# Two norms of an encoder trunk: buffers for the squares, held conditioning chunks, and a fused modulation on VectorE

## The chip, the core and the metric

One core of a Trainium2 chip runs the whole program. The metric is the device time of one execution in microseconds (us), lower is better. TensorE (PE in the profile, PEld where it loads weights) multiplies matrices, VectorE (DVE) and ScalarE (ACT) work on elements, SyncE (SP) issues the DMAs that bring the weights.

## What is computed

A trunk of two layers over 256 tokens of width 1024, all in float32. Each layer is a token mixer and then a feed-forward part, and ahead of each stands a norm whose scale and shift come from a conditioning vector `c`. Cut to what matters here:

```python
def adaln(x, g, shift, scale):
    return rmsnorm(x, g) * (1 + scale[:, None, :]) + shift[:, None, :]
...
    for l in range(DEPTH):
        mod = jax.nn.silu(c) @ ada_w[l] + ada_b[l]
        sh_m, sc_m, g_m, sh_f, sc_f, g_f = jnp.split(mod, 6, axis=-1)
        hn = adaln(x, mix_norm_g[l], sh_m, sc_m)
        ...                                   # four kinds of attention on hn @ w_in[l]
        x = x + g_m[:, None, :] * y
        hn = adaln(x, ffn_norm_g[l], sh_f, sc_f)
        if l % 2 == 0:
            f = swiglu(hn, ffn_w1[l // 2], ffn_w3[l // 2], ffn_w2[l // 2])
        else:
            f = moe_swiglu(...)               # router, 8 experts
        x = x + g_f[:, None, :] * f
    return rmsnorm(x, final_norm_g)
```

## The kernel before, in words

**Layout and precision.** The residual stream `xT` lies transposed in SBUF, eight pieces `xT[:, k]` of 128 channels by 256 tokens. Each float32 operand of a large product is split into a rounded part and the rest (`hi` and `lo` of weights, `hnh` and `hnl` of the normed stream), and `mm3` (matmuls on L102) makes three products of them: hi with hi, lo with hi, hi with lo. A weight comes in loads of 1 MB into a ring of six buffers `raw`; ACT rounds it (`CAST`, L76) and DVE takes the rest (L81), 1024 columns at a time, into four buffers.

**A norm edge.** Between a product and the next one that needs the normed stream stands this chain. DVE adds the gated product to `xT` (L735, eight steps). ACT squares each piece (`Stats.add`, L272); the squares go in pairs into two buffers `sq`, so the fifth square waits until the first pair has been summed. PE sums each square over the channels, two matmuls with one column `mean` per piece. A matmul here of float32 operands stands in the trace as two of half the work, so 16 sums are 32 rows there. From the sums `rsqrt` makes `rtok` (L255 to L259, two steps on ACT, three on DVE), and `Stats.rstd` (L288) spreads it over the partitions with PE, into PSUM. Then `scaled` (L294, DVE) multiplies `xT[:, k]` by it into `hn`, and `modulate` makes of each `hn` the rounded `hnh` (L315, ACT), the same unrounded (L316, ACT) and their difference `hnl` (L317, DVE), with scale `modA` (from `gain`, L303) and shift from `mods`.

There are three such edges and the MoE's own norm: edge 0 at the start, edge 1 between the first mixer and the dense feed-forward part, edge 2 between that and the second mixer.

**Conditioning chunks.** The product of `silu(c)` with `ada_w` is cut into chunks of 512 columns, spread over the program (`Beside.step`): two loads of 1 MB each, and either 32 small matmuls on PE (L215, `pj<-raw,cq`) or, `summed`, eight steps on DVE (L206 and seven of L208) and four matmuls. Each then takes a copy on ACT (L218), a transpose on PE (L219) and an addition on DVE (L221) into `mods`. At edge 1 `beside.upto(0, 10)` makes the chunk whose result `gain` needs; the first summed chunk of the dense part stands close behind it.

**Order.** Each engine runs its instructions in one fixed order. It is set ahead of time by a scheduler that takes instructions as their operands become ready in its own simulated time; `after(inst)` (L62) holds an instruction back behind another. So a local edit can move instructions elsewhere. The dense part is 11 steps of `hidden` (products with `w1` and `w3`) and `down` (with `w2`); the eight experts of the second layer follow much later (from 590 us).

Of the kernel before, what the change touches and what calls it, by code (L numbers as in the profile page):

```python
# [10 lines left out]
F32 = mybir.dt.float32  # L11
# [9 lines left out]
P = 128  # L21
# [18 lines left out]
def trunk(ctx, tc, I, out):  # L40
# [53 lines left out]
    class Acc:  # L94
# [4 lines left out]
            self.first = True  # L99

        def mm(self, o, lhsT, rhs, stop=False):
            pe.matmul(o, lhsT, rhs, start=self.first, stop=stop, skip_group_check=True)  # L102
            self.first = False

        def mm3(self, o, s, m, stop=False):
            self.mm(o, s[0], m[0])
# [44 lines left out]
    class Ada:  # L151
# [33 lines left out]
        def step(self):  # L185
            m, kh, w = self.load()
            for r in range(4):
                self.add(m, cz[:, kh * 4 + r], w[:, r], not self.todo and r == 3)
            if not self.todo:
                self.finish()  # L190

    class Beside:
# [3 lines left out]
            self.todo = list(chunks)  # L196
            self.tag = "pj"

        def step(self, summed=False):

            l, m = self.todo.pop(0)
            ws = [load(rows(I["ada_w"][l], kh * 512, 4, m * 512, m * 512 + 512), 4, 512) for kh in range(2)]
            w = [ws[k // 4][:, k % 4] for k in range(KC)]
            v = main.tile([P, 512], F32, name="ada", bufs=2)
            if summed:
                dve.tensor_scalar_mul(v, w[0], cs[:, 0:1])  # L206
                for k in range(1, KC):
                    dve.scalar_tensor_tensor(v, w[k], cs[:, k:k + 1], v, op0=ALU.mult, op1=ALU.add)  # L208
                terms = [(oz, v)]
            else:  # L210
                terms = [(cq[:, k], w[k]) for k in range(KC)]
            b = bank(self.tag)
            for i, (z, x) in enumerate(terms):
                for j in range(4):
                    pe.matmul(b[32 * j:32 * j + 32, :P], z, x[:, j * P:j * P + P], start=(i == 0),  # L215
                              stop=(i == len(terms) - 1), skip_group_check=True, tile_position=(0, 32 * j))
            v = v[:, :P]
            act.copy(v, b[:, :P])  # L218
            pe.transpose(b[:, P:2 * P], v, ident)  # L219
            a = S_AB + 48 * l + 4 * m  # L220
            dve.tensor_add(mods[l][:, m], b[:, P:2 * P:32], sm[:, a:a + 4])  # L221

        def upto(self, l, m):

            while self.todo and self.todo[0] < (l, m):
                self.step()

    beside = Beside([(0, m) for m in range(4, 12)] + [(1, m) for m in range(12)])
    owed = [0]

    def fill(n=1, summed=False):

        owed[0] += n
        while owed[0] >= 2:
            owed[0] -= 2
            if beside.todo:
                beside.step(summed)

    def mod(l, i):
        return mods[l].rearrange("p m j -> p (m j)")[:, 8 * i:8 * i + 8]  # L240
# [21 lines left out]
    class Stats:  # L262
# [3 lines left out]
            self.nk, self.n, self.tag, self.ms = nk, 0, tag, Acc(tag)  # L266

        def add(self, x):
            if self.n % 2 == 0:
                self.sq = main.tile([P, 2 * T], F32, name="sq", bufs=2)  # L270
            sq = self.sq[:, self.n % 2 * T:][:, :T]
            self.last = act.activation(sq, x, AF.Square)  # L272
            self.n += 1
            for t in range(2):
                self.ms.mm(self.ms.t[:, t:t + 1], sq[:, t * P:t * P + P], mean, self.n == self.nk)

        def tokens(self):

# [12 lines left out]
    def scaled(rstd, dst=None):  # L291
        for k in range(KC):
            t = main.tile([P, T], F32, name="hn", bufs=4) if dst is None else dst[:, k]
            dve.tensor_mul(t, xT[:, k], rstd)  # L294
            yield t
# [33 lines left out]
    def run(steps):  # L329
        for _ in steps:  # L330
            pass

    def ada(chunks):
        a = Ada(0, chunks, "sc")
        while a.todo:
            a.step()
# [19 lines left out]
    def mixer(l, wk, ts):  # L356
        w_in = I["w_in"][l]
        lam_init = 0.8 - 0.6 * math.exp(-0.3 * l)
        (hh, hl), edge = halves(), []
        adaln = modulate(l, S_MG + 8 * l, 0, 1, ts, hh, hl, edge, l == 0)  # L360
        if l == 0:
            ada(range(0, 4, 2))
            next(adaln)
        else:
            run(adaln)

        def hx(k, t0=0, t1=T):
            return hh[:, k, t0:t1], hl[:, k, t0:t1]
# [369 lines left out]
            yield st, k  # L738

    def normed(steps):  # L740
        for st, _ in steps:
            pass
        return scaled(st.rstd())

    def mix_out(l, oTh, oTl, tag=None):
        accs = [Acc("pj") for _ in range(4)]
# [9 lines left out]

    def dense(l, wk, ts):
        (hh, hl), edge = halves(), []
        run(modulate(l, S_FG + 8 * l, 3, 4, ts, hh, hl, edge))
        accs = [Acc(t) for t in ("sc", "sc", "tp", "tp")]  # L760
        ys = [accs[k // 2].t[:, (k % 2) * T:(k % 2) * T + T] for k in range(KC)]
        nst = D_FF // 256
# [31 lines left out]
        for s in range(nst):  # L794
            if s + 1 < nst:
                hidden(s + 1)
            down(s)
            fill(1 if s > 7 else 2, True)
        beside.upto(1, 4)
        return add_gated(ys, mod(l, 5), "pj")  # L800

    with tc.tile_pool(name="wk", bufs=1) as wk:
        mq = wk.tile([P, 8, T], F32, name="mq")
        dve.memset(mq, 0.0)
        o = mixer(0, wk, xn)
        beside.upto(0, 6)
        ts = normed(mix_out(0, *o, "tp"))
        beside.upto(0, 10)
        ts = normed(dense(0, wk, ts))
        o = mixer(1, wk, ts)  # L810
        beside.upto(1, 6)

# [461 lines left out]
```

## Time and profile before

| | |
|---|---|
| median of three executions | 1616.28 us (1615.56 to 1616.67) |
| the profiled execution | 1615.89 us, of which the span of the trace is 1614.1 |
| edge 0 | 0 to 30 us |
| first mixer | 30 to 181.5 us |
| edge 1 | 181.5 to 205 us |
| dense feed-forward part | 205 to 393.5 us |
| edge 2 | 393.5 to 407 us |
| experts | 590 to 1600 us |

The stages are read from the timeline by their lines. The profiled execution is 0.39 us below the median. Where PE is busy all through a stage, the stage ends when PE is done; where PE stands idle, another engine or a transfer sets the time.

### The profile page before, as it was taken

To read this page: it belongs to the slowest core of one execution; us is meant where nothing else is said; L and a number is where in the kernel's file an instruction comes from. 1 tells how busy PE (TensorE), PEld (TensorE's weight loads), DVE (VectorE), ACT (ScalarE), POOL (GpSimd) and SP (SyncE) were. 2 spreads that over 40 slices of the span, in tenths; PEclk is the share of its full clock that TensorE was granted. 3 is DMA by queue.
4 is the path that set the end of the run, shared out by engine and by line. 5 is a ranking of instruction groups with operands and counts; after the bars stand their busy time and mean duration, and the time that the engine had idled before them with its cause. 6 is when DMAs were issued, how large, how long until landed. Compare 5 with 4: busy or idle time off the path is not lost.

```text
span 1614.1 us, 24569 instructions
## 1 busy us (share of the span) xinstructions
PE 1550.2 (96%) x9449; PEld 1314.0 (81%) x9449; DVE 1301.3 (81%) x1840; ACT 1062.0 (66%) x1470; POOL 49.0 (3%) x48
## 2 busy tenths in 40 slices
PE   6999999999999969899999999999999999999997
PEld 5998899999998858787787888878887878788785
DVE  4786577776696489799889999888988888888887
ACT  3666454344766468677677777777777777676775
POOL 0000000000001010000000000000000001000000
PEclk8999899999999979999999999999999999999999
DMA  9874477886573549999989999989998989999992
GB/s 349 308 248 168 160 261 266 299 303 207 185 265 121 207 166 352 319 368 324 349 319 347 370 373 318 385 311 339 363 365 315 378 286 361 338 368 338 354 317 84
DMA packets 224396, 478.31 MB, mean 296 GB/s; under 512 B 11664, under 2 KB 39440, under 8 KB 224272
## 3 DMA queue, kind: packets, MB, share of 16 engines
q1 hardware_dynamic: 224272, 476.68, 82.7%
q8 instruction: 75, 1.23, 0.3%
q14 instruction: 49, 0.40, 0.1%
HBM read 475.60 MB, written 1.05 MB: 295 GB/s over the span
## 4 chain that ended last, share of the span: by engine, by line
PE 53%; DVE 4%; issue 1%; ACT 1%; POOL 0%; ACTq 0%; DVEq 0%
PE pj L102 33%; PE sc L102 17%; DVE mlo L81 2%; PE tp L1026 1%; DVE lo L81 1%; PE tp L102 1%; DVE acc L1072 1%; POOL ada L1063 0%; DVE rs L1059 0%; DVE ada L112 0%; ACT hi L76 0%; ACT mhi L76 0%; PE tp L998 0%; DVE sq L1020 0%; DVE raw L1185 0%
## 5 line engine op out<-in xcount | busy, mean ns | idle before, releaser
L81 DVE TENSOR_TENSOR lo<-raw,hi 128x1024 fp32r<-128x1024 f32 x352 | 423.4, 1223 | 69.1 <-ACT hi L76 63.9
L76 ACT CAST hi<-raw 128x1024 fp32r<-128x1024 f32 x354 | 364.9, 1048 | 102.8 <-PE pj L102 50.6
L81 DVE TENSOR_TENSOR mlo<-raw,mhi 128x1024 fp32r<-128x1024 f32 x224 | 268.4, 1229 | 17.7 <-ACT mhi L76 15.8
L76 ACT CAST mhi<-raw 128x1024 fp32r<-128x1024 f32 x224 | 229.2, 1050 | 39.4 <-PE pj L102 22.8
L102 PE MATMUL pj<-hnh,hi 128*128 128x256 f32 x640 | 182.9, 287 | 3.1 <-ACT hnh L315 2.2
L102 PE MATMUL pj<-hnl,hi 128*128 128x256 f32 x640 | 180.5, 283 | 1.0 <-DVE hnl L317 0.9
L102 PE MATMUL pj<-hnh,lo 128*128 128x256 f32 x640 | 179.2, 282 | 0.3 <-DVE lo L81 0.3
L102 PE MATMUL sc<-hi,ada 128*128 128x512 f32 x448 | 146.6, 398 | 1.6 <-DVE ada L112 1.3
L81 DVE TENSOR_TENSOR mlo<-more,mhi 128x1024 fp32r<-128x1024 f32 x112 | 135.7, 1238 | 14.7 <-ACT mhi L76 14.0
L81 DVE TENSOR_TENSOR lo<-more,hi 128x1024 fp32r<-128x1024 f32 x110 | 131.4, 1220 | 16.8 <-ACT hi L76 9.5
L102 PE MATMUL sc<-mhi,ada 128*128 128x512 f32 x432 | 139.6, 394 | 5.5 <-DVE ada L112 4.1
L76 ACT CAST mhi<-more 128x1024 fp32r<-128x1024 f32 x112 | 115.5, 1051 | 26.6 <-PE pj L102 17.8
L76 ACT CAST hi<-more 128x1024 fp32r<-128x1024 f32 x110 | 113.0, 1050 | 27.4 <-PE pj L102 9.9
L102 PEld LDWEIGHTS pj<-hnh,hi 128*128 128x128 f32 x640 | 121.2, 190 | 8.6 <-issue 3.6
L102 PEld LDWEIGHTS pj<-hnl,hi 128*128 128x128 f32 x640 | 120.6, 189 | 2.6 <-DVE hnl L317 2.0
L102 PEld LDWEIGHTS pj<-hnh,lo 128*128 128x128 f32 x640 | 120.4, 189 | 1.0 <-DVE lo L81 0.6
L102 PE MATMUL pj<-mhi,oTh 128*128 128x512 f32 x336 | 111.9, 402 | 4.4 <-ACTq L1169 4.4
L102 PE MATMUL pj<-hi,oTh 128*128 128x512 f32 x336 | 110.8, 396 | 0.0
L102 PE MATMUL pj<-mhi,oTl 128*128 128x512 f32 x336 | 109.3, 395 | 0.0
L102 PE MATMUL pj<-hi,oTl 128*128 128x512 f32 x336 | 108.0, 392 | 0.2 <-ACT hi L76 0.2
L102 PEld LDWEIGHTS sc<-hi,ada 128*128 128x128 f32 x448 | 84.6, 189 | 23.1 <-DVE ada L112 2.2
L102 PEld LDWEIGHTS sc<-mhi,ada 128*128 128x128 f32 x432 | 80.8, 188 | 24.7 <-DVE ada L112 5.3
(367 smaller groups left out, 3084.1 us busy)
## 6 DMA issues: line engine op xcount, KB each, us to landing
raw<-in_moe_w_dram SPq DMA_DIRECT2D x224, 1024.0 KB, 6.4
more<-in_moe_w_dram SPq DMA_DIRECT2D x111, 1024.0 KB, 6.4
raw<-in_ada_w_dram SPq DMA_DIRECT2D x48, 1024.0 KB, 7.6
raw<-in_ffn_w_dram SPq DMA_DIRECT2D x33, 1024.0 KB, 5.5
raw<-in_w_in_dram SPq DMA_DIRECT2D x22, 1024.0 KB, 7.7
raw<-in_w_out_dram SPq DMA_DIRECT2D x8, 1024.0 KB, 6.0
raw<-in_x_dram SPq DMA_DIRECT2D x1, 1024.0 KB, 5.3
raw<-in_w_in_dram SPq DMA_DIRECT2D x2, 512.0 KB, 7.2
```

Source lines behind the costliest of these rows:

```text
L76: self.last = act.copy(hi, v[:, k:k + n])
L81: dve.tensor_sub(lo, v[:, k:k + n], hi.bitcast(F32))
L102: pe.matmul(o, lhsT, rhs, start=self.first, stop=stop, skip_group_check=True)
L1026: pe.transpose(b[:, j], g[:, j * P:j * P + P], ident)
L1072: dve.scalar_tensor_tensor(d, a[t].t, G[:, t, e:e + 1], d, op0=ALU.mult, op1=ALU.add)
```

## The change

**Squares** (`Stats.add`): the fifth to eighth go into the four buffers of `hn`, so none waits for a pair to be summed. **Chunks**: `Stats.add` now keeps the last sum matmul as `summed`, and at edge 1 the chunk's small matmuls are held behind it (`upto(0, 10, summed)`); the DVE steps of the dense part's first summed chunk are held behind the last `hnl` step of edge 1 (`late`). **Modulation** (`renorm`, edges 1 and 2): DVE makes `w = (xT * A) * rstd` in one step straight from PSUM, ACT makes `hnh = round(w + shift)` in one step, DVE makes `hnl = (w + shift) - hnh` in one step. The second ACT step of each piece is gone (16 in all), `gain` is one step instead of two, and DVE's two steps per piece are both `SCALAR_TENSOR_TENSOR`. Edge 0 keeps `modulate`, and the MoE's norm is not touched.

```diff
         def mm(self, o, lhsT, rhs, stop=False):
-            pe.matmul(o, lhsT, rhs, start=self.first, stop=stop, skip_group_check=True)
+            i = pe.matmul(o, lhsT, rhs, start=self.first, stop=stop, skip_group_check=True)
             self.first = False
+            return i
...
-        def step(self, summed=False):
+        def step(self, summed=False, late=None):
...
             if summed:
-                dve.tensor_scalar_mul(v, w[0], cs[:, 0:1])
+                with after(late):
+                    dve.tensor_scalar_mul(v, w[0], cs[:, 0:1])
...
                 for j in range(4):
-                    pe.matmul(b[32 * j:32 * j + 32, :P], z, x[:, j * P:j * P + P], start=(i == 0),
-                              stop=(i == len(terms) - 1), skip_group_check=True, tile_position=(0, 32 * j))
+                    with after(None if summed or i else late):
+                        pe.matmul(b[32 * j:32 * j + 32, :P], z, x[:, j * P:j * P + P], start=(i == 0),
+                                  stop=(i == len(terms) - 1), skip_group_check=True, tile_position=(0, 32 * j))
...
         def add(self, x):
-            if self.n % 2 == 0:
-                self.sq = main.tile([P, 2 * T], F32, name="sq", bufs=2)
-            sq = self.sq[:, self.n % 2 * T:][:, :T]
+            if self.n >= 4:
+                sq = main.tile([P, T], F32, name="hn", bufs=4)
+            else:
+                if self.n % 2 == 0:
+                    self.sq = main.tile([P, 2 * T], F32, name="sq", bufs=2)
+                sq = self.sq[:, self.n % 2 * T:][:, :T]
...
+    def renorm(l, gcol, ish, isc, rstd, hi, lo, edge):
+
+        A, B = main.tile([P, 8], F32, name="modA", bufs=2), mod(l, ish)
+        gain(A, l, gcol, isc, 0, 8)
+        for k in range(KC):
+            w = main.tile([P, T], F32, name="hn", bufs=4)
+            dve.scalar_tensor_tensor(w, xT[:, k], A[:, k:k + 1], rstd, op0=ALU.mult, op1=ALU.mult)
+            a = act.activation(hi[:, k], w, AF.Identity, bias=B[:, k:k + 1])
+            b = dve.scalar_tensor_tensor(lo[:, k], w, B[:, k:k + 1], hi[:, k].bitcast(F32), op0=ALU.add,
+                                         op1=ALU.subtract)
+            if k == EDGE:
+                edge[:] = b, a
+        return b
...
-        run(modulate(l, S_FG + 8 * l, 3, 4, ts, hh, hl, edge))
+        late = renorm(l, S_FG + 8 * l, 3, 4, ts, hh, hl, edge)
...
-            fill(1 if s > 7 else 2, True)
+            fill(1 if s > 7 else 2, True, late if s == 0 else None)
...
-        ts = normed(mix_out(0, *o, "tp"))
-        beside.upto(0, 10)
-        ts = normed(dense(0, wk, ts))
+        ts, summed = normed(mix_out(0, *o, "tp"))
+        beside.upto(0, 10, summed)
+        ts, _ = normed(dense(0, wk, ts))
```

**PE at edge 1.** These are PE's instructions from the last product of the first mixer to the first of the dense part; x9 counts equal ones in a row. Before:

```order
L102 MATMUL pj<-oTh,lo 128x256
L215 MATMUL pj<-raw,cq 32x128 x9
L102 MATMUL tp<-mean,sq 128x1 x6
L215 MATMUL pj<-raw,cq 32x128
L102 MATMUL tp<-mean,sq 128x1 x2
L215 MATMUL pj<-raw,cq 32x128 x12
L102 MATMUL tp<-mean,sq 128x1 x2
...
L102 MATMUL tp<-mean,sq 128x1 x4
L215 MATMUL pj<-raw,cq 32x128 x5
L219 MATMUL pj<-ident,ada 128x128
L288 MATMUL tp<-ident,rtok 128x128 x2
```

And now, with the line numbers of the changed file:

```order
L102 MATMUL pj<-oTh,lo 128x256
L102 MATMUL tp<-mean,sq 128x1 x8
L102 MATMUL tp<-mean,hn 128x1 x8
L218 MATMUL pj<-raw,cq 32x128 x24
L294 MATMUL tp<-ident,rtok 128x128 x2
L218 MATMUL pj<-raw,cq 32x128 x8
L222 MATMUL pj<-ident,ada 128x128
L102 MATMUL pj<-hnh,hi 128x256 x2
```

The 32 chunk matmuls, which lay among the 16 sums, now follow them, eight of them behind the spreading of `rtok`.

**DVE at edge 1.** These are DVE's instructions from `rtok` on. Before:

```order
L259 SCALAR_TENSOR_TENSOR rtok<-rs 128x2
L221 TENSOR_TENSOR mods_96<-pj,sm 128x4
L303 SCALAR_TENSOR_TENSOR modA<-mods_96,sm 128x4
L206 TENSOR_SCALAR ada<-raw,cs 128x512
L208 SCALAR_TENSOR_TENSOR ada<-raw,cs,ada 128x512
L294 TENSOR_TENSOR hn<-xT,tp 128x256
L208 SCALAR_TENSOR_TENSOR ada<-raw,cs,ada 128x512
L294 TENSOR_TENSOR hn<-xT,tp 128x256
L208 SCALAR_TENSOR_TENSOR ada<-raw,cs,ada 128x512
L317 TENSOR_TENSOR hnl<-hn,hnh 128x256
```

And now:

```order
L224 TENSOR_TENSOR mods_96<-pj,sm 128x4
L309 SCALAR_TENSOR_TENSOR modA<-mods_96,sm 128x8
L318 SCALAR_TENSOR_TENSOR hn<-xT,modA,tp 128x256 x4
L320 SCALAR_TENSOR_TENSOR hnl<-hn,mods_96,hnh 128x256 x3
L318 SCALAR_TENSOR_TENSOR hn<-xT,modA,tp 128x256
L320 SCALAR_TENSOR_TENSOR hnl<-hn,mods_96,hnh 128x256
L318 SCALAR_TENSOR_TENSOR hn<-xT,modA,tp 128x256 x3
L320 SCALAR_TENSOR_TENSOR hnl<-hn,mods_96,hnh 128x256
L81 TENSOR_TENSOR lo<-raw,hi 128x1024 x2
L320 SCALAR_TENSOR_TENSOR hnl<-hn,mods_96,hnh 128x256 x3
L208 TENSOR_SCALAR ada<-raw,cs 128x512
L81 TENSOR_TENSOR lo<-raw,hi 128x1024
```

The eight steps of the summed chunk, which lay between the steps of the norm, stand behind its last `hnl`.

**DVE in the sixth expert.** `ada<-tp,ada` is the rest of a split whose products PE makes next, `acc` the weighted sum of the experts, L81 the rest of a weight. Before:

```order
L81 TENSOR_TENSOR lo<-more,hi 128x1024 x4
L1020 TENSOR_TENSOR sq<-pj,sq 128x512
L1072 SCALAR_TENSOR_TENSOR acc<-tp,G,acc 128x512 x2
L81 TENSOR_TENSOR mlo<-raw,mhi 128x1024 x4
L112 TENSOR_TENSOR ada<-tp,ada 128x512
```

And now:

```order
L1093 SCALAR_TENSOR_TENSOR acc<-tp,G,acc 128x512 x2
L81 TENSOR_TENSOR mlo<-raw,mhi 128x1024 x3
L1041 TENSOR_TENSOR sq<-pj,sq 128x512
L1093 SCALAR_TENSOR_TENSOR acc<-tp,G,acc 128x512 x2
L81 TENSOR_TENSOR mlo<-raw,mhi 128x1024
L113 TENSOR_TENSOR ada<-tp,ada 128x512
```

Here `sq<-pj,sq` stands three weight steps further back. Over the whole program 12 of the 55 `ada` steps stand behind one to eight more weight steps than before (39 in all) and one behind one fewer, most of them from this expert on; up to here PE's order in the experts is as before.

## Rows read from the trace of the kernel before

**Rows 1.** The page: busy time, share of the span and instructions of each engine.
```profile
PE 1550.2 (96%) x9449; PEld 1314.0 (81%) x9449; DVE 1301.3 (81%) x1840; ACT 1062.0 (66%) x1470; POOL 49.0 (3%) x48
```

**Rows 2.** Windows: stretch, length, busy (xinstructions) PE PEld DVE ACT POOL, PEclk, DMA, GB/s.
```profile
181.50:205.00 23.50, 18.64 (x149) 15.10 (x149) 15.97 (x36) 13.68 (x27) 0.00 (x0) 0.78 0.62 206
205.00:393.50 188.50, 188.32 (x1622) 184.27 (x1621) 138.87 (x196) 86.07 (x122) 0.00 (x0) 1.00 0.81 277
393.50:407.00 13.50, 11.18 (x89) 9.63 (x90) 5.69 (x18) 7.16 (x18) 0.00 (x0) 0.62 0.10 39
590.00:1600.00 1010.00, 990.72 (x4413) 802.65 (x4411) 892.94 (x887) 743.51 (x821) 27.52 (x14) 0.99 0.93 338
```

**Rows 3.** Timeline of edge 1, PE and PEld: start, length, count, [idle before, releaser].
```profile
182.54 1.42 PEld L102 LDWEIGHTS tp<-mean,sq 128*128 128x128 f32 x12 [0.20 <-issue]
...
184.84 0.86 PE L215 MATMUL pj<-raw,cq 128*32 128x128 f32 x24
...
187.40 1.46 PE L102 MATMUL tp<-mean,sq 128*128 128x1 f32 x8
...
190.47 1.06 PE L288 MATMUL tp<-ident,rtok 128*128 128x128 f32 x4
...
193.28 0.80 PE L102 MATMUL pj<-hnh,hi 128*128 128x256 f32 x2 [1.75 <-ACT hnh L315]
```

**Rows 4.** Timeline of edge 1, DVE and ACT.
```profile
181.30 1.65 DVE L735 SCALAR_TENSOR_TENSOR xT<-pj,mods,xT 128x256 f32<-128x256 f32 x4
...
189.82 0.16 DVE L259 SCALAR_TENSOR_TENSOR rtok<-rs 128x2 f32<-128x2 f32 x1
189.89 0.27 ACT L218 COPY ada<-pj 128x128 f32<-128x128 f32 x1 [0.49 <-PE pj L215]
...
190.92 0.16 DVE L303 SCALAR_TENSOR_TENSOR modA<-mods,sm 128x4 f32<-128x4 f32 x1
...
192.18 0.41 DVE L294 TENSOR_TENSOR hn<-xT,tp 128x256 f32<-128x256 f32 x1
...
200.41 2.35 DVE L81 TENSOR_TENSOR lo<-raw,hi 128x1024 fp32r<-128x1024 f32 x2
...
204.48 0.75 DVE L317 TENSOR_TENSOR hnl<-hn,hnh 128x256 fp32r<-128x256 f32 x2
```

**Rows 5.** Windows of both edges, and of L102 alone at edge 1.
```profile
187.94:198.06 10.12, 7.46 (x36) 6.12 (x36) 7.58 (x20) 5.20 (x12) 0.00 (x0) 0.50 0.74 260
396.10:406.30 10.20, 7.88 (x56) 6.79 (x56) 3.67 (x12) 5.15 (x13) 0.00 (x0) 0.50 0.01 2
...
193.00:198.06 5.06, 4.22 (x16) 3.69 (x17) 0.50 0.72 254
198.06:205.00 6.94, 4.75 (x31) 3.73 (x30) 1.00 0.67 213
```

**Rows 6.** Timeline of edge 2.
```profile
396.07 3.38 PE L102 MATMUL pj<-mean,sq 128*128 128x1 f32 x16
...
403.93 1.93 PE L215 MATMUL pj<-raw,cq 128*32 128x128 f32 x30
...
405.78 0.29 PEld L102 LDWEIGHTS pj<-hi,hnl 128*128 128x128 f32 x1 [0.38 <-issue]
...
407.26 0.19 PEld L102 LDWEIGHTS pj<-hi,hnl 128*128 128x128 f32 x1 [0.20 <-DVE hn L294]
...
408.50 0.19 PEld L102 LDWEIGHTS pj<-hi,hnl 128*128 128x128 f32 x1 [0.20 <-issue]
```

**Rows 7.** Groups by form, 181 to 394 us: count, busy, mean ns, idle before.
```profile
L208 DVE SCALAR_TENSOR_TENSOR ada<-raw,cs,ada 128x512 f32<-128x512 f32 x70 | 52.3, 747 | 1.7 <-DMA raw<-in_ada_w_dram 1.2
```

**Rows 8.** Weights of the dense part: two issues, a cast, and the page's time to landing.
```profile
199.85 3.31 SPq L59 DMA_DIRECT2D raw<-in_ffn_w_dram  x2
...
220.50 1.06 ACT L76 CAST hi<-raw 128x1024 fp32r<-128x1024 f32 x1
...
raw<-in_ffn_w_dram SPq DMA_DIRECT2D x33, 1024.0 KB, 5.5
```

**Rows 9.** Timeline of edge 0: PE's conditioning product and what it waits for.
```profile
27.66 1.94 PE L172 MATMUL sc<-raw,oTl 128*32 128x128 f32 x32 [1.08 <-DMA raw<-in_ada_w_dram]
```

More of the change, by code (lines that the diff above doesn't have):

```diff
@@ L221, in step, with upto, fill @@
             dve.tensor_add(mods[l][:, m], b[:, P:2 * P:32], sm[:, a:a + 4])
-        def upto(self, l, m):
+        def upto(self, l, m, late=None):
             while self.todo and self.todo[0] < (l, m):
-                self.step()
+                self.step(late=late)
     beside = Beside([(0, m) for m in range(4, 12)] + [(1, m) for m in range(12)])
     owed = [0]
-    def fill(n=1, summed=False):
+    def fill(n=1, summed=False, late=None):
         owed[0] += n
@@ L236, in fill @@
             if beside.todo:
-                beside.step(summed)
+                beside.step(summed, late)
     def mod(l, i):
@@ L274, in add @@
             for t in range(2):
-                self.ms.mm(self.ms.t[:, t:t + 1], sq[:, t * P:t * P + P], mean, self.n == self.nk)
+                self.summed = self.ms.mm(self.ms.t[:, t:t + 1], sq[:, t * P:t * P + P], mean, self.n == self.nk)
         def tokens(self):
@@ L359, in mixer @@
         (hh, hl), edge = halves(), []
-        adaln = modulate(l, S_MG + 8 * l, 0, 1, ts, hh, hl, edge, l == 0)
         if l == 0:
+            adaln = modulate(l, S_MG + 8 * l, 0, 1, ts, hh, hl, edge, True)
             ada(range(0, 4, 2))
@@ L364, in mixer @@
         else:
-            run(adaln)
+            renorm(l, S_MG + 8 * l, 0, 1, ts, hh, hl, edge)
         def hx(k, t0=0, t1=T):
@@ L742, in normed @@
             pass
-        return scaled(st.rstd())
+        return st.rstd(), st.summed
     def mix_out(l, oTh, oTl, tag=None):
```

## The prediction, made before the changed kernel had run

> **What bounds the kernel now.** I read the page first: PE is busy 96% of the span [rows 1], so time can only come from stretches in which PE stands idle or runs at a low clock. The windows by stage then say where these are. In the dense part PE is busy 188.32 of 188.5 us at clock 1.00; at edge 1 it is busy 18.64 of 23.5 us at a mean clock of 0.78, and at edge 2 11.18 of 13.5 at 0.62 [rows 2]. Last I read the timeline of each edge, to see which wait ends last. At edge 1 the chain is PE (sums), ACT and DVE (`rtok`), PE (spreading and the chunk), DVE (`gain`, then the norm's steps). DVE makes the last `hnl` step end at 205.23 (two steps from 204.48, 0.75 us) [rows 4], while PE, fed piece by piece, starts 16 + 31 = 47 products from 193 to 205 [rows 5]. At the pace of the dense part, 1622 in 188.5 us or 0.116 each [rows 2], they would need only 5.5 us. So the end of edge 1 is set by DVE's list, and its start by the sums.
>
> **Squares and the held chunk, edge 1.** Before, the sums start at 182.54 [rows 3], behind nine chunk matmuls (18 rows of 0.04), so PE was free at 181.8; the last eight rows run from 187.40 to 188.86 [rows 3]; chunk matmuls and waits for `sq` lie between. Now all 32 rows of sums can follow each other. Twelve took 1.42 us of weight loading [rows 3], 0.118 each, so 32 take 3.8 us: from 181.8 to 185.6, 3.3 us earlier. The pieces come at a pace of 0.40 us [rows 4], two in 0.80, and the eight rows of two take 0.94, so PE does not wait for them.
>
> The chunk then stands whole behind the sums: 64 rows, 48 of them ahead of the spreading. At full clock 24 rows took 0.86 us [rows 3], about 0.033 each, so 48 take 1.6; at half clock 30 took 1.93 [rows 6], 0.064 each, so 48 take 3.1. `rtok` (1.12 us after the last sum, 188.86 to 189.98 by [rows 3, 4]) ends meanwhile. Then come the spreading, 1.06 us [rows 3], the last 16 rows with a gap of 0.2, 1.2 us at half clock, and the copy, transpose, addition and `gain`: from 189.89 to 191.08 [rows 4], 1.2 us with the step to DVE. Behind a sum that ends at S, the first `w` therefore starts at S + 0.2 + 3.1 + 1.06 + 1.2 + 1.2, S + 6.8, at half clock.
>
> **When the clock falls** is the open number. It stood at 0.50 from 187.94 to 198.06 at edge 1 and from 396.10 to 406.30 at edge 2 [rows 5]. At edge 1 chunk matmuls lay among the sums, and it fell only with the last eight rows of sums [rows 3]; at edge 2 sixteen rows stood alone, and the next sixteen already ran at half clock, in 3.38 us, 0.21 each [rows 6]. Edge 1 now looks like edge 2. If the clock falls after sixteen rows as there, at 183.7, the other sixteen take 3.4 us: S is 187.1 and the first `w` starts at 193.9. If it falls at 187.9 as before, the 48 rows run at full clock and the first `w` starts at 185.6 + 5.3 = 190.9. Between these I take a fall as the sums end: 185.6 + 6.8 = 192.4.
>
> The Trainium skill speaks against this change here ("TensorE: Matmul & The Clock Gate", section "What's actually happening"): the throttled clock is the default and activity releases it, so taking the chunk's matmuls out of the sums takes activity away. This trace agrees in direction: the clock fell sixteen rows into the sums at edge 2 [rows 6] and with the last eight at edge 1 [rows 3]. By that rule alone the first `w` would be the late one, 193.9 and not 190.9, and the sum rival 1's.
>
> **DVE's list at edge 1.** Before, from the first `hn` at 192.18 to 205.23 it takes 13.05 us [rows 4], with seven chunk steps of 0.75 [rows 7] and three L81 in it. Now it holds 16 `SCALAR_TENSOR_TENSOR` and two L81 of 1.18 (2.35 for two, [rows 4]). No row shows these steps on three operands with PSUM and a column; the nearest is L735, also `SCALAR_TENSOR_TENSOR` with one PSUM operand and a column, four in 1.65 us [rows 4], a pace of 0.40 (a bound below is 0.34, two `hnl` steps in 0.75 [rows 4] with the last 0.42 long; above, 0.48, a full step). That makes 6.4 + 2.4 = 8.8 us (7.8 to 10.0). ACT has one step per piece now, so `hnh` is never late for `hnl`. The last `hnl` ends at 192.4 + 8.8 = 201.2, and PE finishes the 47th product about 0.3 later: at the pace of 0.21 up to 198 (about 22 from 193.4) and 0.116 after it, PE alone would be done at 200.9, so DVE still ends last. 205.0 - 201.5 = **3.5 us gained**; with the early and the late fall 2.0 and 5.0 (203.0, 200.0).
>
> **The moved chunk of the dense part** costs DVE 0.5 + 7 x 0.75, 5.7 us, behind the last `hnl`. DVE is busy 138.87 of 188.5 there [rows 2], so 50 us of idle time hide it. Its two ring buffers come free later: before, two loads of weights are issued at 199.85, and the first cast of these loads that I find runs at 220.50 [rows 8]. Now the chunk ends near 209; loads issued then land after 5.5 us [rows 8], at 215. Taken as 0, with 5 us of cover; past that each us late is a us lost, up to all of the gain (rival 2).
>
> **Edge 2.** Sums: no chunk stands among them, and PE runs them without a gap, so the buffers give nothing (0 to 0.1). Norm: PE waits for pieces, 0.38 at 405.78, 0.20 at 407.26 and 0.20 at 408.50 [rows 6]; two DVE steps of 0.40 with one ACT step of 0.50 per piece, instead of two of 0.50, take these away: 0.8, and with pieces so close that no product starts late 1.0. Clock: the second 16 rows take 3.38 us, at full clock 16 x 0.118 = 1.9; a fall later than before gives up to 1.5, an equal one 0. Since before's fall lies near the earliest, I take 0.5. **1.5 us gained** (0.4 to 2.5).
>
> **Edge 0** gets the buffers only. PE waits there for a transfer (1.08 us, `ada_w`, [rows 9]); an earlier sum only waits longer: 0 (-0.5 to +1.0). **Experts**: no instruction of theirs is edited; 12 `ada` steps stand behind more weight steps. DVE has 117 us idle of 1010 [rows 2]: 0 (2 either way).
>
> **Sum**: 3.5 + 1.5 = 5.0. The profiled execution took 1615.89, so 1610.9; the median lies 0.39 higher, so **1611.3 us**. 0.2% of this, 3.2 us, is about what a measurement of this kernel can tell from no change: faster is below 1613.05, slower above 1619.5.
>
> **Rivals.** *1, the clock falls early and the gain is small.* Fall at 183.7: 2.0 at edge 1, and at edge 2 only two gaps, 0.6: 1616.28 - 2.6 = 1613.7. For it: edge 2's rows [rows 6]. Against: the fall came at different points of the two edges [rows 3, 6], so an early one is not given at both. *2, given back in the dense part.* The chunk's buffers or its place on DVE delay a weight; PE, busy 188.32 of 188.5, shows each us at once. If a weight that PE needs comes 5 us behind its need (10 later than worked out above), all is given back: 1616.3, no change. For it: the loads at 199.85 waited for just this buffer [rows 8]. Against: the 5 us of cover. *3, slower.* In the experts the moved `ada` steps make PE wait for weight steps of 1.2 us. If each of the 12 costs one, 14.4 us: 1625.7; it decides from seven on (8.4 us: 1619.7). For it: the order, where these steps lie next to weight steps of the same engine. Against: DVE's 117 us of idle time [rows 2]. *4, the clock hardly falls.* Then chunk, spreading and the last rows run at full clock, `w` starts near 189.9 and edge 1 gives 6.0; edge 2 gives 2.5: 1607.8. That the fused steps do nothing is no case apart: the list of 13.05 us holds 5.25 of chunk steps that are gone from it either way.
>
> **How the numbers follow.** Forecast 0.54 (its own range 1609 to 1613), rival 1 0.14, rival 2 0.13, rival 3 0.10, rival 4 0.09. Faster: 0.52 of the forecast, 0.09, and 0.04 of rival 1: 0.65. Same: 0.02, 0.10 and 0.13: 0.25. Slower: 0.10. The range from 1607.0 to 1615.0 leaves out rival 3 and most of rival 2: about 0.2.
>
> **What would show it.** Right: the sums in one run of about 3.8 to 5 us from 181.8; the first `w` between 190.9 and 193.9; `hn` and `hnl` steps at a pace of 0.40; the last `hnl` 8.8 us behind the first `w`; no idle PE from 205 on; at edge 2 no gaps behind the first products. Wrong: a first `w` behind 194, `hnl` waiting for ACT, PE idle between 203 and 225 for a cast or an L81, or experts longer by more than 2 us.

## The result and the profile after

The changed kernel takes 1599.01 us (median of four, 1597.79 to 1602.59) against 1616.47 for the kernel before in the same runs (1615.56 to 1617.91): a ratio of 0.9898, with a 95% interval of 0.9883 to 0.9913. That is 17.5 us faster; 5.0 were forecast, and the time lies 8 us below the range that was stated. The profiled execution took 1598.14 us. One of the eight executions of late_only below took 3943.68 us at a granted clock of 0.386: its median counts it, its ratio does not.

The page, the row of busy times that answers to [rows 1], shows PE with 9.4 us less to do for the same 9449 matmuls, and the mean granted clock of that execution is 0.984 against 0.979, so part of the gain is a higher clock:

```profile
span 1596.4 us, 24570 instructions
...
PE 1540.8 (97%) x9449; PEld 1310.6 (82%) x9449; DVE 1305.7 (82%) x1838; ACT 1060.1 (66%) x1454; POOL 46.6 (3%) x48
```

The windows of edge 1, the dense part and edge 2 answer to [rows 2], each cut where the stage now begins and ends:

```profile
181.70:199.90 18.20, 15.06 (x145) 13.57 (x144) 11.23 (x29) 10.02 (x20) 0.00 (x0) 0.81 0.40 143
199.90:388.50 188.60, 188.60 (x1630) 184.49 (x1629) 145.58 (x204) 85.47 (x122) 0.00 (x0) 1.00 0.84 289
388.50:401.00 12.50, 10.21 (x90) 8.93 (x90) 7.85 (x22) 6.56 (x17) 0.00 (x0) 0.73 0.10 37
```

The dense part has no idle PE, and DVE carries the moved chunk there (145.58 us busy). The timeline of PE at edge 1 answers to [rows 3]:

```profile
181.86 1.84 PE L102 MATMUL tp<-mean,sq 128*128 128x1 f32 x16
183.57 1.93 PE L102 MATMUL tp<-mean,hn 128*128 128x1 f32 x16
185.43 2.60 PE L218 MATMUL pj<-raw,cq 128*32 128x128 f32 x48
187.96 1.23 PE L294 MATMUL tp<-ident,rtok 128*128 128x128 f32 x4
189.11 0.64 PE L218 MATMUL pj<-raw,cq 128*32 128x128 f32 x16
...
191.99 0.51 PE L102 MATMUL pj<-hnh,hi 128*128 128x256 f32 x2 [1.51 <-ACT hnh L319]
```

All 32 rows of sums run at full clock and end at 185.5, as forecast. DVE's list, which answers to [rows 4], starts at 190.91 and ends at 199.57 (198.30 + 1.27), 8.66 us long; 8.8 was forecast:

```profile
186.45 0.16 DVE L262 SCALAR_TENSOR_TENSOR rtok<-rs 128x2 f32<-128x2 f32 x1
...
190.91 1.65 DVE L318 SCALAR_TENSOR_TENSOR hn<-xT,modA,tp 128x256 f32<-128x256 f32 x4
192.48 1.27 DVE L320 SCALAR_TENSOR_TENSOR hnl<-hn,mods,hnh 128x256 fp32r<-128x256 f32 x3
...
196.03 2.35 DVE L81 TENSOR_TENSOR lo<-raw,hi 128x1024 fp32r<-128x1024 f32 x2
198.30 1.27 DVE L320 SCALAR_TENSOR_TENSOR hnl<-hn,mods,hnh 128x256 fp32r<-128x256 f32 x3
```

The clock at edge 1, which answers to [rows 5], was low in two pieces with full clock between (start:end, length, busy times, clock):

```profile
185.80:189.20 3.40, 3.40 (x52) 2.79 (x48) 0.48 (x3) 0.20 (x1) 0.00 (x0) 0.52 0.17 31
189.20:192.60 3.40, 1.39 (x19) 0.72 (x19) 2.02 (x7) 1.44 (x4) 0.00 (x0) 0.99 1.02 387
192.60:196.00 3.40, 2.99 (x14) 2.99 (x15) 3.40 (x9) 2.35 (x5) 0.00 (x0) 0.51 0.52 199
```

So edge 1 went by the steps that were forecast, but by the table below the two edges won 8.1 us where 5.0 were forecast. Where the rest came from is seen when PE's matmuls are numbered in order of time, from 0: every profile records 9449, so the time from the start of one number to the start of another is the same amount of PE work in every kernel, up to its order. From such differences comes this table of the profiled executions (us between two numbers; the experiments' rows are used below):

| kernel | edge 1, 1700 to 1975 | edge 2, 3450 to 3800 | branch, 5290 to 5340 | 7800 to 7960 | 8430 to 8520 | 6900 to 8520 |
|---|---|---|---|---|---|---|
| before | 38.2 | 44.0 | 18.3 | 39.7 | 24.6 | 369.8 |
| before_again | 40.6 | 42.5 | 18.2 | 39.7 | 24.5 | 369.8 |
| pool_step_on_dve | 40.3 | 42.8 | 17.8 | 39.7 | 24.3 | 369.5 |
| buffers_only | 43.5 | 41.7 | 18.0 | 36.6 | 20.0 | 364.8 |
| late_only | 37.9 | 41.7 | 17.7 | 37.2 | 20.0 | 365.8 |
| hold_only | 38.3 | 41.6 | 18.2 | 36.6 | 20.0 | 363.9 |
| renorm_only | 39.2 | 41.6 | 15.7 | 36.6 | 20.0 | 364.0 |
| hold_and_late | 33.1 | 42.6 | 17.9 | 36.6 | 20.0 | 363.9 |
| late_and_renorm | 36.5 | 41.6 | 15.4 | 37.3 | 20.5 | 366.3 |
| no_late | 35.9 | 40.3 | 16.9 | 39.7 | 21.1 | 365.8 |
| no_renorm_edge1 | 35.0 | 41.8 | 17.7 | 36.6 | 20.0 | 365.0 |
| no_renorm_edge2 | 33.8 | 41.8 | 17.9 | 36.6 | 20.0 | 363.9 |
| no_buffers | 33.6 | 41.8 | 13.8 | 36.6 | 20.0 | 364.0 |
| act_pad8 | 33.8 | 41.8 | 18.1 | 36.6 | 20.0 | 366.4 |
| act_pad16 | 33.9 | 41.8 | 18.2 | 36.6 | 20.0 | 364.0 |
| after_again | 34.1 | 40.2 | 14.9 | 36.6 | 20.0 | 363.9 |
| after | 33.4 | 40.7 | 15.5 | 36.6 | 20.0 | 363.9 |

Of the 17.7 us between the first and the last row's executions, edge 1 gives 4.8, edge 2 3.3 and the dense part 0.5 (171.9 to 171.4 between 1975 and 3450). Another 9.6 come in the experts, where nothing was edited: 2.8 at a branch within the first of them (at 648 us), 0.9 between 5340 and 6900 (a stretch of half clock from 802.3 to 805.7 us is gone), and 5.9 between 6900 and 8520, where the order of the experts' instructions is another: PE's parts from that of before at number 6836 (1004.6 us), ahead of the sixth expert already. About 0.5 is lost at edge 0 and in the mixers.

### The profile page after: what moved, and what is told of

Its sections match the earlier page's. It is cut to its first block, busy times and chain, and to the rows that moved or that the text cites. A ratio compares the mean times of both kernels' runs of the same rounds, so it can differ in the third digit from the quotient of the medians.

```text
span 1596.4 us, 24570 instructions
## 1 busy us (share of the span) xinstructions
PE 1540.8 (97%) x9449; PEld 1310.6 (82%) x9449; DVE 1305.7 (82%) x1838; ACT 1060.1 (66%) x1454; POOL 46.6 (3%) x48
## 4 chain that ended last, share of the span: by engine, by line
PE 52%; DVE 5%; issue 1%; ACT 1%; ACTq 0%; DVEq 0%
PE pj L102 32%; PE sc L102 18%; DVE mlo L81 2%; DVE lo L81 2%; PE tp L1047 1%; PE tp L102 1%; DVE acc L1093 1%; ACT mhi L76 0%; DVE ada L113 0%; DVE sq L1041 0%; DVE rs L1080 0%; ACT hi L76 0%; DVE rs L1002 0%; DVE st L1020 0%; ACT ada L1083 0%
## 5 line engine op out<-in xcount | busy, mean ns | idle before, releaser
L81 DVE TENSOR_TENSOR lo<-raw,hi 128x1024 fp32r<-128x1024 f32 x352 | 424.4, 1223 | 69.1 <-ACT hi L76 64.8
L81 DVE TENSOR_TENSOR mlo<-raw,mhi 128x1024 fp32r<-128x1024 f32 x224 | 270.0, 1229 | 21.3 <-ACT mhi L76 18.1
L102 PE MATMUL pj<-hnh,hi 128*128 128x256 f32 x640 | 182.2, 287 | 1.5 <-ACT hnh L319 1.5
L102 PE MATMUL pj<-hnl,hi 128*128 128x256 f32 x640 | 180.0, 283 | 1.2 <-DVE hnl L320 1.2
L102 PE MATMUL pj<-hnh,lo 128*128 128x256 f32 x640 | 179.1, 282 | 0.0
L81 DVE TENSOR_TENSOR lo<-more,hi 128x1024 fp32r<-128x1024 f32 x110 | 132.8, 1228 | 19.0 <-ACT hi L76 11.8
L102 PE MATMUL sc<-hi,ada 128*128 128x512 f32 x448 | 145.8, 396 | 2.6 <-DVE ada L113 1.7
L81 DVE TENSOR_TENSOR mlo<-more,mhi 128x1024 fp32r<-128x1024 f32 x112 | 134.7, 1228 | 13.4 <-ACT mhi L76 12.2
L102 PE MATMUL sc<-mhi,ada 128*128 128x512 f32 x432 | 139.4, 394 | 4.2 <-DVE ada L113 3.5
L76 ACT CAST hi<-more 128x1024 fp32r<-128x1024 f32 x110 | 114.0, 1050 | 29.1 <-PE pj L102 14.0
L102 PEld LDWEIGHTS pj<-hnh,hi 128*128 128x128 f32 x640 | 121.1, 190 | 6.4 <-issue 4.2
L102 PEld LDWEIGHTS pj<-hnl,hi 128*128 128x128 f32 x640 | 121.0, 189 | 2.0 <-DVE hnl L320 1.7
L102 PEld LDWEIGHTS pj<-hnh,lo 128*128 128x128 f32 x640 | 120.5, 189 | 0.6 <-issue 0.4
L102 PE MATMUL pj<-mhi,oTh 128*128 128x512 f32 x336 | 110.9, 399 | 2.9 <-PEq L1190 2.9
L102 PE MATMUL pj<-hi,oTh 128*128 128x512 f32 x336 | 110.3, 395 | 0.0
L102 PE MATMUL pj<-mhi,oTl 128*128 128x512 f32 x336 | 108.9, 395 | 0.0
L102 PE MATMUL pj<-hi,oTl 128*128 128x512 f32 x336 | 107.8, 392 | 0.0
L102 PEld LDWEIGHTS sc<-hi,ada 128*128 128x128 f32 x448 | 84.0, 188 | 24.1 <-DVE ada L113 3.0
L102 PEld LDWEIGHTS sc<-mhi,ada 128*128 128x128 f32 x432 | 80.9, 188 | 23.3 <-DVE ada L113 4.6
```

The lines of the kernel that those rows point to most:

```text
L76: self.last = act.copy(hi, v[:, k:k + n])
L81: dve.tensor_sub(lo, v[:, k:k + n], hi.bitcast(F32))
L102: i = pe.matmul(o, lhsT, rhs, start=self.first, stop=stop, skip_group_check=True)
```

## The experiments

Theory A: the gain behind 590 us comes from the order of the experts' instructions, which the scheduler gives as soon as edge 1 changes. Theory B: it comes from the edges, by an earlier arrival. Theories C and D are on what carries edge 1, E and F on the branch.

**One part alone, and all but one.** These are the parts that differ from the kernel before or from the changed one.

late_only (before, with the held dense chunk):

```diff
-            fill(1 if s > 7 else 2, True)
+            fill(1 if s > 7 else 2, True, late if s == 0 else None)
```

> The kernel before with one part of the change alone: the eight DVE steps of the dense part's first summed chunk are held behind the last hnl of edge 1. On PE and DVE the experts' instructions then stand in the order of the changed kernel. Theory A (the 9.6 us that the changed kernel wins behind 590 us come from the experts' order, which any edit ahead of them flips): edge 1 ends about 3 us earlier (seven chunk steps of 0.75 out of DVE's list, less what the sums still cost), the experts win 8 to 10: 1603 to 1606 us. Theory B (they come from the edges, by an earlier arrival and its transfers): the experts win under 3 us: 1611 to 1614.

Measured: 1608.49 us, 0.9961 of before (0.9947 to 0.9975).

no_late (the changed kernel, with that line undone):

```diff
-            fill(1 if s > 7 else 2, True, late if s == 0 else None)
+            fill(1 if s > 7 else 2, True)
```

> The changed kernel without the hold of the dense part's first summed chunk, all else as changed. The chunk's steps stand among the norm's steps again, and the experts' order lies nearer to that of before (216 of the last 5800 PE instructions differ from it, against 578). Theory A (order): edge 1 wins 0 to 2 us, edge 2 about 2.8, the experts 0 to 4: 1608 to 1613 us. Theory B (edges): the experts win about as much as in the changed kernel: 1601 to 1605.

Measured: 1603.21 us, 0.9930 (0.9911 to 0.9950). A's times were missed, because the edges won more than it said (edge 1 2.3 against the first profile of before, edge 2 3.7) and the experts the upper end, 4.0. The time lies in B's range, but behind 590 us this kernel won 5.3 (1.4 at the branch, 4.0 in the experts), not about as much as the changed kernel's 9.6.

hold_only (before, with the chunk of edge 1 held):

```diff
-        beside.upto(0, 10)
+        beside.upto(0, 10, summed)
```

> The kernel before with the chunk of edge 1 alone held behind the last sum. Squares still wait for their two buffers, and the DVE list is as before. The experts' order is that of the changed kernel but for two instructions on DVE and two on ACT. Theory A (order): edge 1 wins 0 to 1.5, the experts 8 to 10: 1605 to 1608.5 us. Theory B (edges): 1614.5 to 1616.5.

Measured: 1605.33 us, 0.9941 (0.9922 to 0.9961).

renorm_only (before, with `renorm` at both edges):

```diff
-            run(adaln)
+            renorm(l, S_MG + 8 * l, 0, 1, ts, hh, hl, edge)
...
-        run(modulate(l, S_FG + 8 * l, 3, 4, ts, hh, hl, edge))
+        renorm(l, S_FG + 8 * l, 3, 4, ts, hh, hl, edge)
```

> The kernel before with the fused modulation alone, at both edges; buffers, chunk and dense chunk as before. The experts' order is that of the changed kernel. Theory A (order): edge 1 wins about 1 (16 steps of 0.40 on DVE in place of 16 of 0.34, but no ACT step in between, the seven chunk steps still in the list), edge 2 about 2.5, the experts 8 to 10: 1602.5 to 1606 us. Theory B (edges): 1611.5 to 1614.

Measured: 1604.68 us, 0.9931 (0.9912 to 0.9950).

Theory B falls here. The three kernels with one part win 0.3, -0.1 and -1.0 us at edge 1 against the first profile of before, and still 4.0 to 5.9 us between 6900 and 8520, in the experts, where nothing is edited. In renorm_only the experts' order is that of the changed kernel, in hold_only all but two instructions of DVE and of ACT, and so are both places, 36.6 and 20.0, to 0.05 us. late_only was expected to have this order too. In its trace 141 of the last 4450 matmuls stand elsewhere, between 1232 and 1300 us; it has 37.2 in the first place, and a stretch of half clock at 1050 us takes part of its gain back. no_late, whose order is nearer to that of before (244 of these matmuls stand elsewhere, 564 against the changed kernel), has 39.7 as before in the one place and 21.1 in the other. Nor does the arrival decide: buffers_only, below, comes to number 5290 later than before (649.1 against 647.1 us) and has 36.6 and 20.0, and no_late comes earlier (640.6) and has 39.7. The times alone would not settle it, since those of hold_only and renorm_only lie in A's ranges, that of late_only between the two, and that of no_late in B's.

**The places themselves.** The timeline of before at the first of them:

```profile
1240.97 3.48 DVE L81 TENSOR_TENSOR mlo<-raw,mhi 128x1024 fp32r<-128x1024 f32 x3
...
1244.37 0.68 DVE L1020 TENSOR_TENSOR sq<-pj,sq 128x512 f32<-128x512 f32 x1
...
1245.11 0.66 PE L1026 MATMUL tp<-ident,sq 128*128 128x128 f32 x4 [1.08 <-DVE sq L1020]
...
1246.10 0.68 DVE L112 TENSOR_TENSOR ada<-tp,ada 128x512 fp32r<-128x512 f32 x1
...
1246.84 0.97 PE L102 MATMUL sc<-mhi,ada 128*128 128x512 f32 x3 [1.08 <-DVE ada L112]
```

Three weight steps stand ahead of `sq` on DVE, PE waits for `sq`, and then for `ada`. In the changed kernel these weight steps stand behind `sq`, and PE waits for neither:

```profile
1232.24 0.68 DVE L1041 TENSOR_TENSOR sq<-pj,sq 128x512 f32<-128x512 f32 x1
...
1233.93 0.60 PE L1047 MATMUL tp<-ident,sq 128*128 128x128 f32 x4
```

The two waits, with one of 0.73 us for ACT just ahead of them, are 2.9 of the 3.1 us that this place gives; 0.2 us of waiting is left there. At the second place, the one in the sixth expert, the timeline of before reads:

```profile
1368.72 6.00 POOL L1063 TENSOR_TENSOR ada<-rs,ada 128x512 fp32r<-128x512 f32 x1 [6.32 <-ACT ada L1062]
1368.96 4.62 DVE L81 TENSOR_TENSOR lo<-more,hi 128x1024 fp32r<-128x1024 f32 x4
...
1374.77 0.73 PE L102 MATMUL tp<-ada,st 128*128 128x512 f32 x2 [2.17 <-POOL ada L1063]
```

A step on GpSimd of 6.00 us holds PE for 2.2 us, and PE then runs at half clock from 1375.7 on (window, length, busy times, clock):

```profile
1375.70:1379.10 3.40, 3.02 (x12) 2.53 (x12) 3.40 (x5) 0.59 (x1) 0.00 (x0) 0.50 0.95 343
```

In the changed kernel the step took 1.81 us, and the clock stayed full:

```profile
1355.37 1.81 POOL L1084 TENSOR_TENSOR ada<-rs,ada 128x512 fp32r<-128x512 f32 x1 [4.49 <-PE tp L102]
```

The two places give 3.1 and 4.6 us. In the rest of 6900 to 8520 the changed kernel is 1.8 us longer, so the new order costs something too.

pool_step_on_dve (before, with this one step on DVE):

```diff
-                    pool.tensor_sub(ol, o, oh.bitcast(F32))
+                    (dve if (e, n) == (5, 1) else pool).tensor_sub(ol, o, oh.bitcast(F32))
```

> The kernel before with one instruction moved from GpSimd to DVE: the rest of a split at the end of the sixth expert, which took 6.00 us on GpSimd in the profile of before while the other thirteen of its kind took 1.3 to 2.0. Edges and everything ahead of that place are as before. Theory A (the experts' gain is in a few places of the order, this one the largest at 4.6 us): 3.5 to 4.6 us are won between 1358 and 1396 us, in all 1610.5 to 1612. Theory B (the gain comes from the edges): this place wins nothing by itself, 1614.5 to 1616.5.

Measured: 1621.04 us, 1.0021 (1.0010 to 1.0031): slower, which neither theory gave. The wait for GpSimd is gone, but the waits of PE in the same stretch now are:

```profile
PE pj L102 <- DVE mlo L81: 2.7, 1, 2.7
```

So the place still takes 24.3 us, and the new order behind it costs 3.8 us between 8900 and 9440 (128.6 against 124.8 in nearly all others), a part of which ran at half clock (1503.4 to 1506.8). So it is not enough to take this one wait away. The edit put a wait of 2.7 us for a weight step in its place, so what the GpSimd step costs by itself is not shown.

before_again (before, unchanged):

> The kernel before, unchanged, with a second profile. Theory A: the places of the experts at 1243 and 1372 us take the same time as in the first profile, within 0.5 us; the stall at 648 us, the low clock at 802 us and the lengths of the low clock at both edges may differ by 1 to 4 us each, as chance. Theory B: the experts take the same time within 1 us everywhere, the stall at 648 us too. Time 1611 to 1619.

Measured: 1616.80 us. The experts' places repeat within 0.1 us and the branch too. Edge 1 took 2.4 us longer and edge 2 1.5 less: the clock stood at half from 185.3 to 202.4 at edge 1, and from 400.3 to 407.1 at edge 2:

```profile
185.30:202.40 17.10, 14.43 (x91) 11.91 (x80) 9.75 (x25) 7.97 (x17) 0.00 (x0) 0.50 0.57 184
400.30:407.10 6.80, 4.48 (x40) 3.39 (x40) 3.38 (x11) 4.19 (x10) 0.00 (x0) 0.51 0.01 2
```

So one profile can't tell 2 us at an edge; the first profile of before had a good edge 1 and a bad edge 2. With the 40.3 of pool_step_on_dve, whose edges are those of before, edge 1 of before took 39.7 us on average.

**What carries edge 1.**

no_buffers (the changed kernel, without the further buffers for squares):

```diff
-            if self.n >= 4:
-                sq = main.tile([P, T], F32, name="hn", bufs=4)
-            else:
```

> The changed kernel without the four further buffers for squares; the experts' order is that of the changed kernel. If the buffers carry the early sums, the sums at edge 1 end 1 to 2.5 us later, and the time is 1600 to 1602 us. If the held chunk alone brings them forward, the time is that of the changed kernel within 0.8 us.

Measured: 1598.70 us, 0.9898 (0.9877 to 0.9919), the time of the changed kernel. The sums run in 3.63 us in one row without the buffers:

```profile
182.21 3.63 PE L102 MATMUL tp<-mean,sq 128*128 128x1 f32 x32
```

buffers_only (before, with these buffers alone):

> The kernel before with the four further buffers for squares alone. DVE's list at edge 1 is as before, so the edge wins 0 to 1.5 us. The experts' order differs from that of the changed kernel in 81 of the last 5800 PE instructions, from that of before in 659. Theory A (order): the experts win 5 to 8, in all 1606 to 1610 us. Theory B (edges): 1614 to 1616.

Measured: 1608.85 us, 0.9950 (0.9933 to 0.9967); edge 1 took 43.5 us in its profile, the longest of all and 20.5 us of it at half clock. That profile, of the slowest of its four executions, shows 5.0 us won by the experts' order and 2.2 at edge 2, where its parts are those of before but for the buffers; a gain of the buffers at edge 1 it does not show.

hold_and_late (before, with the edits of hold_only and of late_only):

> The kernel before with both holds (the chunk of edge 1 behind the sums, the dense chunk behind the last hnl), without buffers and without the fused steps. The experts' order is that of the changed kernel (but for two instructions on DVE and two on ACT), worth about 6 us. Theory C (edge 1 needs early sums and a short DVE list together): edge 1 wins 2.5 to 4 us, edge 2 0 to 2 as chance of the clock: 1604 to 1607 us. Theory D (the fused steps carry edge 1): edge 1 wins 0 to 1.5: 1607 to 1610.

Measured: 1601.77 us, 0.9914 (0.9892 to 0.9936), below C's range because edge 1 won 5.1 us and the dense part another 1.4. late_and_renorm (before, with the edits of late_only and of renorm_only; the chunk of edge 1 lies among the sums):

> The kernel before with the fused steps at both edges and the dense chunk held, but the chunk of edge 1 among the sums again and no further buffers. The experts' order differs from that of the changed kernel in 213 of the last 5800 PE instructions. Theory C: the sums end late, the first w starts at 193 to 195, DVE's list of 8.8 us ends at 202 to 204, edge 1 wins 1 to 3, edge 2 1 to 2.5, the experts 5 to 7: 1604 to 1608 us. Theory D: edge 1 wins 4 to 6: 1600 to 1603.

Measured: 1601.57 us, 0.9908 (0.9885 to 0.9931). The time is D's, but edge 1 won 1.7 us, as C says; the rest is edge 2 (2.4), the dense part (1.8), the branch (2.9) and the experts (3.5). no_renorm_edge1 (the changed kernel with the old steps at edge 1, its `renorm` line undone):

> The changed kernel with the three old steps per piece at edge 1; edge 2 keeps the fused ones. Experts' order as changed. Theory C: edge 1 wins 2.5 to 4 instead of 5 to 6: 1600.5 to 1603 us. Theory D: edge 1 wins 0 to 1.5: 1603 to 1605.5. If the fused steps give nothing at edge 1: 1598 to 1600.

Measured: 1602.14 us, 0.9915 (0.9894 to 0.9936), in C's range; edge 1 won 3.3 us in its profile. no_renorm_edge2 (the same for edge 2):

> The changed kernel with the three old steps per piece at edge 2; edge 1 keeps the fused ones. Experts' order as changed. If the fused steps are worth the 1.0 us of the forecast at edge 2 (the rest of the 2.8 measured there being the clock): 1599.5 to 1601 us. If all of 2.8 us is theirs: 1601 to 1603. Edge 1 and the experts as in the changed kernel by either.

Measured: 1602.72 us, 0.9922 (0.9901 to 0.9943). Of the 3.7 us that it lies above the changed kernel, its profile shows 2.3 at the branch and 1.1 at edge 2, so the time does not show that all of 2.8 us is theirs, though it lies in the range given for that.

Theory C stands and D falls. Against the mean of 39.7 us for before, one hold alone wins 1.4 or 1.8 us at edge 1 (38.3 and 37.9), the buffers alone nothing (43.5), the fused steps alone no more than the noise (39.2), and both holds together, without the fused steps, 6.6 (33.1). Whether the fused steps add anything on top is open: with both holds edge 1 takes 33.4 to 34.1 us with them (six profiles) and 33.1 and 35.0 without. PE at edge 1 in hold_and_late:

```profile
182.36 3.63 PE L102 MATMUL tp<-mean,sq 128*128 128x1 f32 x32
185.92 2.01 PE L218 MATMUL pj<-raw,cq 128*32 128x128 f32 x48
187.85 1.22 PE L294 MATMUL tp<-ident,rtok 128*128 128x128 f32 x4
189.01 1.08 PE L218 MATMUL pj<-raw,cq 128*32 128x128 f32 x16
190.23 0.50 PE L102 MATMUL pj<-hnh,hi 128*128 128x256 f32 x2
```

Its first product starts at 190.23, 1.8 us ahead of the changed kernel's 191.99: the old `hn` needs `rtok` alone, the fused `w` needs `gain` as well, behind the whole chunk. But DVE's list is longer in hold_and_late; its first step and its last:

```profile
189.12 0.75 DVE L300 TENSOR_TENSOR hn<-xT,tp 128x256 f32<-128x256 f32 x2 [2.01 <-PE tp L294]
...
200.60 0.42 DVE L337 TENSOR_TENSOR hnl<-hn,hnh 128x256 fp32r<-128x256 f32 x1 [0.36 <-ACT hn L336]
```

It ends at 201.02, 18.7 us behind the start of the sums, in the changed kernel 17.7 us behind it. The clock differed as well: hold_and_late had half clock for 3.4 us (186.8 to 190.2), the changed kernel for 6.8.

How long the half clock lasts at edge 1 is not all chance: it goes with the place of the chunk. In the ten profiles with the chunk held behind the sums it lasted 3.4 to 10.2 us in all and the clock first rose again at 188.3 to 190.4, while PE ran the chunk or just behind it. In the seven with the chunk among the sums it lasted 10.2 to 20.5 us, and the clock first rose at 192.0 to 203.2.

At edge 2 the kernels with the fused steps there took 40.2 to 41.8 us, those with the old ones 41.6 to 44.0. The half clock lasted about 6.8 or about 10.2 us there. Where it lasted 6.8, the means are 40.4 (three profiles) and 42.0 (six), where 10.2, they are 41.7 (six) and 43.3 (two). So about 1.6 us is the fused steps', and the longer half clock costs 1.3.

**The branch.** In the first expert each engine jumps over code for a rare case (L1169 before, L1190 after). The rows of the branch and of the first step behind it on PE's and ACT's queues (count: min/median/max ns, first and last start us), of before and of the changed kernel:

```profile
L1169 ACTq COMPARE_BRANCH  x1: 50/50/50, 648.3 to 648.3; - x1
L1169 PEldq EVENT_SEMAPHORE  x1: 51/51/51, 651.1 to 651.1; - x1
L1169 ACTq EVENT_SEMAPHORE  x1: 17/17/17, 653.2 to 653.2; - x1
```

```profile
L1190 ACTq COMPARE_BRANCH  x1: 50/50/50, 640.2 to 640.2; - x1
L1190 ACTq EVENT_SEMAPHORE  x1: 17/17/17, 640.6 to 640.6; - x1
L1190 PEldq EVENT_SEMAPHORE  x1: 51/51/51, 643.5 to 643.5; - x1
```

Before, ACT goes on 4.9 us behind its branch and PE waits for it; after, it goes on after 0.4 us, and PE's own branch is the later one. Of all kernels up to here, the short wait is found in those with the fused steps at both edges and in no other.

act_pad16 and act_pad8 (the changed kernel with 16 and with 8 steps more on ACT):

```diff
+        pad = wk.tile([P, 16], F32, name="pad")
+        for i in range(16):
+            act.copy(pad[:, i:i + 1], epst)
```

> The changed kernel with 16 copies of one column on ACT near the start, where ACT waits for transfers; every other instruction stands as in the changed kernel. Theory E (at the branch on the count of tokens ACT goes on after 0.4 us only in the kernels in which both edges use the fused steps, because its program is 16 instructions shorter there, and after 4.6 to 5.7 us in all others): ACT goes on 4.5 to 6 us behind its branch again, the stretch of PE's products 5290 to 5340 takes 17.5 to 18.5 us instead of 13.8 to 15.7, and the time is 1600.5 to 1603 us. Theory F (the short wait comes from an earlier arrival or by chance): ACT goes on after 0.4 us, 1598 to 1600.

> The same with 8 copies, so that ACT has as many instructions as the kernels with the fused steps at one edge. Theory E: ACT goes on 4.5 to 6 us behind its branch, 1600 to 1603 us. Theory F: after 0.4 us, 1598 to 1600.

> The changed kernel, unchanged, with a second profile. Theory E: ACT goes on after 0.4 us. By chance alone it would be long in most programs. Edge 1 and 2 together within 2 us of the first profile, by the clock; the places of the experts within 0.3 us; 1597 to 1603 us.

Measured: 1605.03 us for act_pad16 (0.9932, 0.9911 to 0.9953), 1607.97 for act_pad8 and 1597.12 for the changed kernel again, the last two in single executions. The branch in act_pad16:

```profile
L1193 ACTq COMPARE_BRANCH  x1: 50/50/50, 643.2 to 643.2; - x1
...
L1193 ACTq EVENT_SEMAPHORE  x1: 17/17/17, 648.1 to 648.1; - x1
```

ACT waits 4.9 us again (4.6 with 8 steps, 0.4 in after_again), and the stretch takes 18.2 us (18.1 and 14.9). Theory E holds: with 8 or 16 steps more ahead of the branch ACT waits again. The arrival does not decide, for renorm_only came to its branch at 647.0 us, later than act_pad16 at 643.2, and waited 0.4. Whether it is the length of ACT's program or the place of the branch in it is not shown. Both kernels lie 2 to 5 us above E's range, since other stretches were longer too: with half clock edge 2 (41.8; 394.2 to 404.5 us in act_pad16), the stretch behind 5340 (354.3 against 353.2; 797.0 to 800.4) and in act_pad8 another 2.5 between 6900 and 7800 (1050.2 to 1057.0). The dense part took 172.5 against 171.4; why was not tried.

## Why the prediction was wrong

**The step that failed** is the one on the experts: "no instruction of theirs is edited ...: 0 (2 either way)". They won 5.9 us by their order, 0.9 by the clock and 2.8 at the branch in the first of them: 9.6 us in all, nearly twice the forecast gain. The reason given for the 0, DVE's 117 us of idle time, is no bound on what PE waits for one step of DVE: [rows 2] has PE idle for 19.3 us of that stage, and no term prices any of it. The order ahead of the prediction showed the moved steps, and the trace of before held the waits that they removed: PE waited 1.08 us for `sq` and as long for `ada` near 1245, and 2.2 us for GpSimd near 1374, with half clock behind it. I counted the moved steps as a danger (rival 3) and priced none of the waits that a new order could end. Rival 3 had the mechanism with the wrong sign; the kernel with one step moved to DVE shows that the other sign exists as well (3.8 us lost in one place).

**Edge 1** went by its steps. The sums ended at 185.5 (185.6 forecast), all of them at full clock. The clock fell at 185.8, where I had taken it, but it was at full clock again from 189.2 to 192.6, and the chunk took less than costed (2.60 us for the first 48 rows, not 3.1, and 0.64 for the last 16, not 1.2), so `w` started at 190.9, the early bound, and not at 192.4. DVE's pace was 0.40 and its list 8.66 us (8.8). The gain was mis-sized for that reason: 4.8 against the first profile of before, about 7 against before_again, where 3.5 was taken and 5.0 was the bound. The part of the Trainium skill ("TensorE: Matmul & The Clock Gate", section "What's actually happening") that spoke against the change was borne out in the fall at 185.8, 2.1 us ahead of before's, but not in the sum: the late first `w`, at 193.9, did not come, and the half clock was shorter with the chunk behind the sums (6.8 us against 10.2), not longer.

Of the parts, the buffers were costed as part of the early sums and give nothing (1598.70 without them). That the fused steps shorten the list is right, but at edge 1 they also wait for `gain`, a wait that I put into the chain without asking whether the old `hn` had it; the profiles with both holds leave them between a loss of 0.7 us and a gain of 1.2 there. That the hold of the chunk shortens the half clock was in no term.

**The moved chunk** cost nothing, as forecast: two loads are issued at 203.36 instead of 199.85, and PE is busy 188.60 of 188.60 us. **Edge 2**: 1.5 forecast, 3.3 measured between the first profiles, of which about 1.6 is the fused steps' by the means above (1.0 forecast for the gaps) and 1.3 the clock's (0.5 forecast), which fell at 394.0, behind the sums, and stayed low for 6.8 us instead of 10.2. **Edge 0**: 0.3 us lost between numbers 0 and 750, within its bounds.

## What to carry to other kernels

An edit in a kernel whose order a scheduler sets is an edit of the whole program: price the waits that stand in the trace behind the edit, since a new order can end them or make others, and compare the order there before calling a stage untouched. Of several parts that look additive at one edge, test pairs: here two holds together won 6.6 us at an edge where each alone won less than 2, and the buffers gave nothing on top. Before ten microseconds are put down to an edit, look at what the same edit does to unrelated places such as a branch.

## What was not expected of the hardware

ACT resumed 0.4 us behind a branch with 1454 recorded instructions, and 4.6 to 4.9 with 8 or 16 more; eight steps of 128x1 near the start moved the wait. Why just this length is short was not settled. The GpSimd step of 128x512 took 6.00 us in one place and 1.3 to 2.0 in the thirteen others of before; it lay beside four weight steps of DVE in a row, but that these caused it was not tried. The half clock at edge 1 lasted from 3.4 us (hold_and_late) to 20.5 in three pieces (buffers_only), and for the same program 10.2 in one execution and 17.1 in another, with 2.4 us between their edges.
